# An account of VectorE's work paces the convolution's taps, pairs step first, and VectorE copies the histories

## The chip, the cores and the metric

The kernel runs on one core of a Trainium2 chip. The core's engines run side by side, each through its own queue in order: TensorE (PE, with its weight loads as PEld), VectorE (DVE), ScalarE (ACT), GpSimd (POOL) and SyncE (SP), which issues the DMAs. The metric is the device time of one execution in microseconds; the lower the better.

## The reference, cut to what matters

One layer of a streaming encoder is computed for 320 tokens: 256 of a prompt and 64 of a running stream, with model width 2048.

```python
h = rmsnorm(x, g_pre_mix)
p = h @ w_in                                   # 6160 columns
a_out, conv_buf = conformer_conv(p[..., :c0], p[..., c0:c1], conv_buf, w_dw, b_dw, gn_g, gn_b)
b_out, qkv_buf, s = gdn_mixer(p[..., c1:c2], p[..., c2:c3], ...)   # 8 heads of 128, gated delta rule
x = x + rmsnorm(jnp.concatenate([a_out, b_out], axis=-1) @ w_out, g_post_mix)
h = rmsnorm(x, g_pre_ffn)
gu, ffn_buf = causal_dwconv(h @ w_up, ffn_buf, w_ffn_dw, b_ffn_dw)
x = x + rmsnorm((jax.nn.silu(gate) * up) @ w_down, g_post_ffn)
```

The part that the change touches is the Conformer convolution: a gated input `u = h_val * sigmoid(h_gate)`, then a causal depthwise convolution over positions with 31 taps, each output needing the 30 positions before it (its history: zeros, or for the running stream a stored state), then a group norm over 128 channels and a swish. Eight groups of 128 channels are eight independent convolutions. The other half is the gated delta rule: per head a short convolution of q, k and v, and a blockwise recurrence in chunks of 64 or 128 tokens with the inverse of a triangular matrix.

## The kernel before, in words

All activations lie with channels on the 128 partitions and the 320 tokens along the free axis. Each weight matrix is cut into blocks of 128 output channels. A block's weights arrive by DMA in two half blocks of 1024 columns (three buffers). ScalarE rounds a half block to a high part (`whi`, line L214) and VectorE computes the rest (`wlo`, L215); TensorE then makes three products for each 128 rows (L230, L231, L234): high by high, high by low, low by high. `block_matmul` does this, and each matmul is counted by `tick`. A block of the input projection has 16 x 3 = 48 ticks.

**The dense plan.** After the first norm, the string PLAN orders the blocks: `h0` to `h7` are heads (q, k and v block each: `gdn_pre`, `qkv_block`), `c0` to `c7` convolutions (gate block and value block: `conv_block`), `z0` to `z7` output gates. Then come the blocks of the output projection (`w_out1`, 33 ticks each), a second part of it (`w_out2`, L1051 to L1053), and the feed-forward layer, which has no part in the change.

**The jobs.** The small work between the blocks is written as Python generators, the jobs. A job yields at each point where its next matmuls would wait for other engines, and names how many ticks later it wants to go on, and how many PSUM banks of two kinds it holds. After every 20 ticks (GAP), `tick` opens a slot: it takes the jobs that are due, in order of their due time, as far as the banks go, and lets each issue its next step right behind the dense matmul. A step that yields with the word "scale" is taken after the others. The jobs are

- `conv_tail` of each convolution: it looks once per slot whether its taps are issued, then transposes (L575), takes statistics (L577 to L584), scales (`un`, L588), transposes back (L592) and applies the swish (`af`, L594, `bh`, L238);
- `gdn_tail` of each head: transposes of q, k and v (L673 to L677), squares on ScalarE (L679, L681), norms on GpSimd (L686 to L692), scaled copies (L696 to L701), and the products `pk` and `pks` (L705, L709) with VectorE's `np` and `at` (L713, L717). Its last step marks the head as done;
- `pair` of each two heads: it looks once per slot whether both heads are marked; `base_inverse` then stores `np` by SP's queue (L729) and inverts small blocks on VectorE (L744 to L758); `levels` widens the inverse in steps of TensorE and ScalarE (`pz` L782, `zh` L783, `px` L788, again with `zq` L807 and `px` L812); `post` runs the recurrence (`pvn` L854, `po` L862, `rhs` L875, `pvns` L883) and ends in `pt_o` (L937) and `zo` (L939).

**The convolution's taps.** `conv_block` evaluates the gate (`sg`, L533) and value (`hv`, L540) and writes `ub` (L541), a tile of five segments of 94 columns: 30 of history and 64 new. ScalarE then copies the stored state and the other segments' histories (L543, L544). `ub` has three buffers, so convolution b takes that of b - 3. The convolution is 31 multiply-adds over 320 columns on VectorE (L557 to L560, in two sums `cvt` and `odd`) and one addition (L554): 32 instructions, which `conv_block` puts into the list `taps`. At the end of a slot `tick` issues the first few of the list, ordered behind the newest VectorE instruction of the slot's jobs. How many is `pace`: 1 while a head's blocks run, 3 in other steps of the plan, 4 after it. `finish_conv(b - 3)` issues what is left of an older convolution before its buffer is written again, and after the plan convolutions 0 to 4 are finished, since `w_out1` reads them.

The order on each engine is set when the program is built: instructions go by their place in the program, minus an offset for those inside `high_priority` (evacuations of PSUM 3000, jobs 1500, weight splits 600, taps none), as their buffers and inputs allow.

Of the kernel before, what the change touches and what calls it, by code (L numbers as in the profile page):

```python
# [22 lines left out]
T = TP + TS  # L23
# [5 lines left out]
HALF = 1024  # L29
NWARM = 8  # L30
GAP = 20
PRI_J = 1500
LAG_GATE = 60
LAG_CONV = 40
# [65 lines left out]
@with_exitstack  # L100
def trunk_kernel(ctx, tc, ins, outs):
    nc = tc.nc
    V, S, G, PE = nc.vector, nc.scalar, nc.gpsimd, nc.tensor
    PRI_W = 600
    boost = [0]
    PRI_E = 3000
# [3 lines left out]

    dense = [None, 0]
    held_t = [0]
    jobs = []


    taps, pace = [], [3]

    def next_tap(front=None):
        left, fn = taps.pop(0)
        with ExitStack() as e:  # L120
            if front is not None:
                e.enter_context(tc.issue_after(front))
            fn()
        left[0] -= 1

    def advance(job, behind=None):
        with tc.issue_after(behind or dense[0]), tc.high_priority(offset=PRI_J):
            try:
                wait, job[2], job[3], *kind = next(job[1])
                job[0] = dense[1] + wait  # L130
                job[4] = kind
            except StopIteration:
                jobs.remove(job)
        return next(i for i in reversed(nc.cur_bb.bb.instructions) if i.engine == dense[0].engine)

    def start(gen, wait, g=0, t=0):
        job = [dense[1] + wait, gen, g, t, []]
        jobs.append(job)
        return job
# [5 lines left out]
    def newest(engine, n0):  # L145
        return next((i for i in reversed(nc.cur_bb.bb.instructions[n0:]) if i.engine == engine), None)

    def tick(mm):
        dense[0] = mm.ins
        dense[1] += 1  # L150
        if dense[1] % GAP == 0:
            g, t0, behind, due = 0, held_t[0], dense[0], []
            t = t0
            n0 = len(nc.cur_bb.bb.instructions)
            for job in sorted(jobs, key=lambda j: j[0]):
                if job[0] <= dense[1] and g + job[2] <= 4 and t + job[3] <= 2:
                    g += job[2]
                    t += job[3]
                    due.append(job)
            for job in due:  # L160
                if not job[4]:
                    behind = advance(job, behind)
            scalar = newest(mybir.EngineType.Activation, n0)
            for job in due:
                if "scale" in job[4]:
                    with ExitStack() as e:
                        if scalar is not None:
                            e.enter_context(tc.issue_after(scalar))
                        advance(job)
            held_t[0] = t - t0  # L170
            front = newest(mybir.EngineType.DVE, n0)
            for _ in range(min(pace[0], len(taps))):
                next_tap(front)

    const = ctx.enter_context(tc.tile_pool(name="const", bufs=1))
# [13 lines left out]
    def pv(name, a=None, b=None):  # L189
        o, w = PAR[name]  # L190
        if a is None:
            return par[:, o:o + w]
        return par[:, o + a:o + (a + 1 if b is None else b)]
# [103 lines left out]
    def in_block(b, name):  # L297
        if b in ready:
            return ready.pop(b)
        ps = ps_p.tile([P, 512], F32, tag="p", name=name)  # L300
        block_matmul(ps[:, 0:T], ins["w_in"][b], hx, (8, 8))
        return ps
# [10 lines left out]
    with tc.tile_pool(name="xp", bufs=1) as xp:  # L313
# [85 lines left out]
        def first_norm():  # L399
            rr, _ = rstd([ssum[:, 0, :], ssum[:, 1, :]])  # L400
            yield 36, 1, 0
            S.copy(rb, rstd_rows(rr)[0])

        job = start(first_norm(), 24, 1)
# [116 lines left out]
    def finish_conv(b):  # L521
        while any(left is lefts[b] for left, _ in taps):
            next_tap()
        finish(convs[b])
# [3 lines left out]
    def conv_block(b):  # L528
        psg_ = in_block(8 + b, "psgate")
        ub = ubufs[b % 3]  # L530
        with tc.high_priority(offset=PRI_E):
            sg = cb.tile([P, T], F32, tag="sg", bufs=1, name="sg")
            V.tensor_tensor(sg, psg_[:, 0:T], rb, ALU.mult)  # L533
            S.activation(sg, sg, AF.Tanh, scale=0.5)
        psv = in_block(b, "psv")
        if b > 2:
            finish_conv(b - 3)
        with tc.high_priority(offset=PRI_E):
            hv = cb.tile([P, T], F32, tag="t320", bufs=2, name="hv")
            V.scalar_tensor_tensor(hv, psv[:, 0:T], 0.5, rb, ALU.mult, ALU.mult)  # L540
            V.scalar_tensor_tensor(ub[:, :, 30:94], sg.rearrange("p (s i) -> p s i", s=5), 1.0,  # L541
                                   hv.rearrange("p (s i) -> p s i", s=5), ALU.add, ALU.mult)
            S.copy(ub[:, 4, 0:30], pv("s_conv", b * 30, (b + 1) * 30))  # L543
            S.copy(ub[:, 1:4, 0:30], ub[:, 0:3, 64:94])  # L544
        for i in range(2):
            nc.sync.dma_start(outs["conv"][:, b, i, :], ub[:, 3 + i, 64:94])

        cvt = cb.tile([P, 5, 64], F32, tag="cvt", bufs=3, name="cvt")
        odd = cb.tile([P, 5, 64], F32, tag="odd", bufs=1, name="odd")
        left = [32]  # L550

        def tap(t):
            if t == 31:
                return lambda: V.tensor_tensor(cvt, cvt, odd, ALU.add)  # L554
            x, acc, w = ub[:, :, t:t + 64], (cvt, odd)[t % 2], pv("w_dw", b * 31 + t)
            if t == 0:
                return lambda: V.tensor_scalar(acc, x, w, pv("b_dw", b), ALU.mult, ALU.add)  # L557
            if t == 1:
                return lambda: V.tensor_scalar(acc, x, w, None, ALU.mult)
            return lambda: V.scalar_tensor_tensor(acc, x, w, acc, ALU.mult, ALU.add)  # L560

        lefts[b] = left
        taps.extend((left, tap(t)) for t in range(32))
        return cvt.rearrange("p s i -> p (s i)"), left

    def conv_tail(b, cvt, left):
        while left[0]:
            yield GAP, 0, 0
        yield LAG_CONV, 0, 1
# [79 lines left out]
    def gdn_tail(h, st, kq, vT):  # L649
        s = h % NS  # L650
        while not gate or (s and "kq" not in st) or (h // NS > 1 and "free" not in sts[h // NS - 2]):
            yield GAP, 1 + 2 * s, 1
        if s == 0:
# [72 lines left out]
    def base_inverse(bt, st):  # L726
# [9 lines left out]
        G.memset(wi_t[:, 0:256:17], 1.0)  # L736
        yield 2 * GAP, 0, 0

        d8, w8 = (t.rearrange("p (b x) -> p b x", b=2)[:, :, 0:128].rearrange("p b (r c) -> p b r c", c=16)[:, :, :, 0:8]
                  for t in (dn_t, wi_t))  # L740
        for r in range(6, -1, -1):
# [5 lines left out]
            if r in (3, 0):  # L747
                yield GAP, 0, 0
        tmp = tmp_t.rearrange("p (r c s) -> p r c s", r=8, c=8)
# [3 lines left out]
        V.tensor_reduce(x, tmp, AX.X, ALU.add)  # L753
        yield GAP, 0, 0
        V.tensor_tensor(tmp, wi[:, 0:8, 0:8].unsqueeze(2).to_broadcast((nb, 8, 8, 8)),
# [195 lines left out]
    def pair(i, st):  # L951
        while any(s not in st for s in range(NS)):
            yield GAP, 0, 0
        yield from base_inverse(i, st)
        yield LAG_BASE - 5 * GAP, 1, 0
        yield from levels(st)
        while i and any(j is pairs[i - 1] for j in jobs):
            yield GAP, 2, 0
        yield LAG_WAIT, 2, 0
        yield from post(i, st)  # L960

    plan = PLAN.split()
    tails, convs, pairs, sts = {}, {}, {}, []
    for step in plan:
        kind, i = step[0], int(step[1:] or 0)
        pace[0] = 1 if kind == "h" else 3
        if kind == "c":
            convs[i] = start(conv_tail(i, *conv_block(i)), GAP)
        elif kind == "g":
            gates_job = start(gates(), 0)  # L970
            advance(gates_job)
        elif kind == "h":
            if i % NS == 0:
                if i:
                    ready[24 + i] = in_block(24 + i, "psq")
                st = {}
                sts.append(st)
                pairs[i // NS] = start(pair(i // NS, st), 0)
            tails[i] = start(gdn_tail(i, st, *gdn_pre(i, st)), LAG_HEAD, 1 + 2 * (i % NS), 1)
        else:  # L980
            z_block(i)
    pace[0] = 4
    for i in range(5):
        finish_conv(i)
    for i in range(3):
# [8 lines left out]
    for n in range(KB - 1):  # L994
        psm = ps_p.tile([P, 512], F32, tag="p", name="psm")
        block_matmul(psm[:, 0:T], ins["w_out1"][n], bx, (6, 5))
        m.append(act.tile([P, T], F32, tag=f"hl{n}", name=f"m{n}"))
        with tc.high_priority(offset=PRI_E):
            S.copy(m[n], psm[:, 0:T])
    while jobs:  # L1000
        advance(jobs[0])
    pa.close()
# [107 lines left out]
    first = up_group()  # L1110
# [13 lines left out]
    job = start(second_norm(), 68, 1)  # L1124
# [29 lines left out]
    for q in range(NQ):  # L1154
# [5 lines left out]
        for j in range(QB):  # L1160
            b = q * QB + j
# [53 lines left out]
    for step in PLAN_Y.split():  # L1215
        how, ks = step[0], step[1:]
        n = 2 if len(ks) == 4 else 1
# [96 lines left out]
```

## Time and profile before

| | |
|---|---|
| median of 3 runs | 1500.84 us (1497.14 to 1501.93) |
| the profiled execution | 1498.26 us, of it the span 1496.5 us |
| TensorE busy | 1480.7 us (99%), 10609 matmuls |
| VectorE busy | 998.4 us (67%) |
| ScalarE busy | 723.7 us (48%) |
| GpSimd busy | 226.4 us (15%) |
| mean granted TensorE clock | 0.998 |

The span is the time from the first to the last instruction that the profiler recorded. A row of an engine's timeline gives its start from the span's beginning, its length, the source line, what it writes and reads, and in square brackets how long the engine stood idle before it and what it waited for. A row of waits gives the engine, what it was about to write, what it waited for, and then the total in us, the number of times and the longest. Lengths of neighbouring rows overlap, since an engine starts an instruction before the one ahead has wholly ended; the distance of two starts is what an instruction costs its queue. L215 and the like are lines of the kernel before.

### The profile page before, as it was taken

Reading aid. Unit: us, or ns where it says so; the run is one execution under the profiler, and the core shown is the slowest. Engines: PE = TensorE matmul, PEld = TensorE weight load, DVE = VectorE, ACT = ScalarE, POOL = GpSimd, SP = SyncE. Lnnn points to the kernel's source line nnn. Section 1 sums busy time; section 2 is a strip of 40 time slices with the busy share of each in tenths; the row PEclk is TensorE's granted clock in tenths of the full one; section 3 lists DMA queues with packets and bytes.
Section 4 is the critical chain, followed back from the end, with each engine's and each line's share of the span. In section 5 each row is a group of like instructions: output and inputs, shape, how many; then the busy total and the mean of one; then the engine's idle time right before and its main releaser. Section 6 shows DMA issues by size and latency. Waiting matters only on the chain.

```text
span 1496.5 us, 27233 instructions
## 1 busy us (share of the span) xinstructions
PE 1480.7 (99%) x10609; PEld 1459.7 (98%) x10610; DVE 998.4 (67%) x1840; ACT 723.7 (48%) x1305; POOL 226.4 (15%) x390
## 2 busy tenths in 40 slices
PE   9999999999999999999999999999999999999998
PEld 8999899989999999999999999999999999999997
DVE  6779886979989678766335666445666545656554
ACT  7664556554544656544434444334444333444453
POOL 0011001120010000332002222002223101223101
PEclk9999999999999999999999999999999999999999
DMA  8435453444434744444554444454444455444453
GB/s 297 134 128 160 137 157 120 131 143 144 130 106 142 226 146 141 154 143 130 154 166 154 149 151 137 138 159 162 152 155 138 136 149 171 154 147 150 131 151 118
DMA packets 98281, 224.22 MB, mean 150 GB/s; under 512 B 18792, under 2 KB 39528, under 8 KB 98152
## 3 DMA queue, kind: packets, MB, share of 16 engines
q1 hardware_dynamic: 98008, 222.45, 47.4%
q8 instruction: 83, 1.36, 0.4%
q14 instruction: 46, 0.38, 0.1%
q10 hardware_dynamic: 144, 0.03, 0.0%
HBM read 215.33 MB, written 7.12 MB: 149 GB/s over the span
## 4 chain that ended last, share of the span: by engine, by line
PE 82%; DVE 9%; ACT 3%; DMA 2%; issue 2%; POOL 1%; ACTq 0%; DVEq 0%; POOLq 0%
PE psu L234 13%; PE psu L231 13%; PE psu L230 13%; PE psdn L230 7%; PE psdn L231 6%; PE psdn L234 6%; DVE wlo L215 3%; PE psq L230 3%; PE psq L231 3%; PE psq L234 3%; PE psu L1107 1%; ACT whi L214 1%; DVE cvt L560 1%; PE ps_first L395 1%; DMA w<-in_w_out 1%
## 5 line engine op out<-in xcount | busy, mean ns | idle before, releaser
L214 ACT CAST whi<-w 128x1024 fp32r<-128x1024 f32 (+2 forms) x440 | 412.9, 940 | 488.4 <-PE psu L231 169.4
L215 DVE TENSOR_TENSOR wlo<-w,whi 128x1024 fp32r<-128x1024 f32 (+2 forms) x440 | 477.3, 1085 | 196.5 <-ACT whi L214 124.7
L231 PE MATMUL psu<-lo,whi 128*128 128x320 f32 x1344 | 397.0, 309 | 0.0
L230 PE MATMUL psu<-hi,whi 128*128 128x320 f32 x1344 | 397.0, 309 | 0.0
L231 PEld LDWEIGHTS psu<-lo,whi 128*128 128x128 f32 x1344 | 252.3, 188 | 0.0
L230 PEld LDWEIGHTS psu<-hi,whi 128*128 128x128 f32 x1344 | 252.3, 188 | 0.0
L234 PE MATMUL psu<-hi,wlo 128*128 128x320 f32 x1344 | 224.4, 309 | 0.0
L234 PEld LDWEIGHTS psu<-hi,wlo 128*128 128x128 f32 x1344 | 204.0, 188 | 0.0
L231 PE MATMUL psdn<-gl,whi 128*128 128x320 f32 x660 | 195.9, 310 | 0.0
L1140 POOL COPY nffn<-fbuf 128x2 f32<-128x2 f32 x88 | 101.5, 1153 | 586.9 <-DVE fbuf L1138 583.7
L1138 DVE TENSOR_TENSOR fbuf<-psu,rb 128x256 f32<-128x256 f32 x88 | 37.4, 425 | 168.9 <-PE psu L234 168.9
L230 PE MATMUL psdn<-gh,whi 128*128 128x320 f32 x480 | 142.8, 309 | 0.0
L231 PEld LDWEIGHTS psdn<-gl,whi 128*128 128x128 f32 x660 | 123.9, 188 | 0.3
L230 PE MATMUL psq<-hh,whi 128*128 128x320 f32 x352 | 106.2, 315 | 0.0
L231 PE MATMUL psq<-hl,whi 128*128 128x320 f32 x352 | 104.1, 309 | 0.0
L230 PEld LDWEIGHTS psdn<-gh,whi 128*128 128x128 f32 x480 | 90.1, 188 | 0.0
L234 PE MATMUL psdn<-gh,wlo 128*128 128x320 f32 x480 | 89.9, 309 | 0.0
L234 PEld LDWEIGHTS psdn<-gh,wlo 128*128 128x128 f32 x480 | 75.3, 188 | 0.0
L230 PEld LDWEIGHTS psq<-hh,whi 128*128 128x128 f32 x352 | 66.1, 188 | 0.3
L231 PEld LDWEIGHTS psq<-hl,whi 128*128 128x128 f32 x352 | 66.1, 188 | 0.2
L560 DVE SCALAR_TENSOR_TENSOR cvt<-ub,par,cvt 128x320 f32<-128x320 f32 x120 | 65.3, 545 | 0.2
L1183 DVE TENSOR_TENSOR y<-y,psdn 128x320 f32<-128x320 f32 x45 | 22.0, 488 | 58.9 <-PE psdn L234 58.9
(357 smaller groups left out, 2479.5 us busy)
## 6 DMA issues: line engine op xcount, KB each, us to landing
w<-in_w_up SPq DMA_DIRECT2D x176, 512.0 KB, 3.6
w<-in_w_in SPq DMA_DIRECT2D x88, 512.0 KB, 3.9
w<-in_w_down SPq DMA_DIRECT2D x64, 384.0 KB, 3.2
w<-in_w_down SPq DMA_DIRECT2D x64, 320.0 KB, 2.9
w<-in_w_out SPq DMA_DIRECT2D x32, 320.0 KB, 3.3
w<-in_w_out SPq DMA_DIRECT2D x16, 384.0 KB, 3.1
w<-in_w_first SPq DMA_DIRECT2D x6, 512.0 KB, 6.5
wtp<-wsp SPq DMA_DIRECT2D x4, 640.0 KB, 5.8
```

Source lines behind the costliest of these rows:

```text
L214: S.copy(hi[:, 0:width], w[:, 0:width])
L215: V.tensor_tensor(lo[:, 0:width], w[:, 0:width], hi[:, 0:width].bitcast(F32), ALU.subtract)
L230: tick(PE.matmul(ps, wh, xh, start=(first and k0 + j == 0), stop=False))
L231: tick(PE.matmul(ps, wh, xl, start=False, stop=False))
L234: tick(PE.matmul(ps, lo[:, j * P:(j + 1) * P], xh, start=False, stop=(final and k0 + j == nk - 1)))
L395: tick(PE.matmul(ps, w, xh, start=(k == 0 and wt is hi), stop=(k == KB - 1 and wt is lo)))
L560: return lambda: V.scalar_tensor_tensor(acc, x, w, acc, ALU.mult, ALU.add)
L1107: PE.matmul(pss[i][:, 0:T], wt[:, o:o + P], x, start=(k == 0 and n == 0), stop=(k == KB - 1 and n == 2))
L1138: V.tensor_tensor(buf[:, 2:258], psu[:, 0:TP], rb2[:, 0:TP], ALU.mult)
L1140: G.tensor_copy(nffn[:, b, 0, :], buf[:, 256:258])
L1183: V.tensor_tensor(y[:, n, :], y[:, n, :], psd[:, 0:T], ALU.add)
```

## The change

- **The account.** All VectorE instructions go through a wrapper, `Counted`, which adds 0.12 us plus 0.00094 us per column to `spent`. At the end of a slot the account's `ends` (when VectorE would be done) is raised to the slot's start if it lies behind it, and `spent` is added; `clock` moves on by V_SLOT = 3.1 us. Taps are then issued as long as the next one would still end by `clock`. The fixed `pace` is gone, in the plan and after it; before the last jobs are run out, all taps that are left are issued.
- **Pairs first.** Of the due jobs of a slot, the pairs' steps are issued first; the choice of the due jobs stays as it was.
- **The histories.** The two copies into `ub` (L543, L544) are VectorE's instead of ScalarE's.

```diff
+V_OP, V_COL = 0.12, 0.00094
+V_SLOT = 3.1
...
-    V, S, G, PE = nc.vector, nc.scalar, nc.gpsimd, nc.tensor
+    S, G, PE = nc.scalar, nc.gpsimd, nc.tensor
+    spent = [0.0]
+    class Counted:
+        def __getattr__(self, name):
+            fn = getattr(nc.vector, name)
+            def run(out, first, *args, **kw):
+                n = first.free_size() if name in ("tensor_reduce", "bn_stats") else out.free_size()
+                spent[0] += V_OP + n * V_COL
+                return fn(out, first, *args, **kw)
+            return run
+    V = Counted()
...
-    taps, pace = [], [3]
+    taps, clock, ends = [], [0.0], [0.0]
...
-            for job in due:
+            for job in sorted(due, key=lambda j: all(j is not p for p in pairs.values())):
                 if not job[4]:
                     behind = advance(job, behind)
...
-            for _ in range(min(pace[0], len(taps))):
+            ends[0] = max(ends[0], clock[0] - V_SLOT) + spent[0]
+            clock[0] += V_SLOT
+            spent[0] = 0.0
+            while taps and ends[0] + spent[0] + V_OP + T * V_COL <= clock[0]:
                 next_tap(front)
...
-            S.copy(ub[:, 4, 0:30], pv("s_conv", b * 30, (b + 1) * 30))
-            S.copy(ub[:, 1:4, 0:30], ub[:, 0:3, 64:94])
+            V.tensor_copy(ub[:, 4, 0:30], pv("s_conv", b * 30, (b + 1) * 30))
+            V.tensor_copy(ub[:, 1:4, 0:30], ub[:, 0:3, 64:94])
...
-        pace[0] = 1 if kind == "h" else 3
...
-    pace[0] = 4
...
+    while taps:
+        next_tap()
     while jobs:
         advance(jobs[0])
```

More of the change, by code (lines that the diff above doesn't have):

```diff
@@ L112, in trunk_kernel @@
     held_t = [0]
-    jobs = []
-    taps, pace = [], [3]
+    jobs, pairs = [], {}
+    taps, clock, ends = [], [0.0], [0.0]
     def next_tap(front=None):
@@ L962, in trunk_kernel @@
     plan = PLAN.split()
-    tails, convs, pairs, sts = {}, {}, {}, []
+    tails, convs, sts = {}, {}, []
     for step in plan:
         kind, i = step[0], int(step[1:] or 0)
-        pace[0] = 1 if kind == "h" else 3
         if kind == "c":
```

## The prediction

> **What bounds the kernel now.** I read the page first, then the busy time by stretch, then the waits of TensorE, and last the order of instructions around each of its waits.
>
> ```profile
> span 1496.5 us, 27233 instructions
> ...
> PE 1480.7 (99%) x10609; PEld 1459.7 (98%) x10610; DVE 998.4 (67%) x1840; ACT 723.7 (48%) x1305; POOL 226.4 (15%) x390
> ```
>
> TensorE is busy for 99% of the span, and the change removes no matmul. All that can be won is TensorE's idle time, and only where the scheduled jobs run, before about 500 us. The next rows are stretches there (us; busy time of PE, PEld, DVE, ACT, POOL; granted clock; DMA), then one plain stretch from the second half of the layer.
>
> ```profile
> core 0: us, PE busy (x) PEld busy (x) DVE busy (x) ACT busy (x) POOL busy (x), PEclk, DMA share, GB/s
> ...
> 151.91:186.53 34.62, 32.53 (x355) 30.84 (x354) 28.93 (x70) 18.40 (x51) 3.60 (x9) 0.95 0.42 136
> ...
> 263.18:308.73 45.55, 45.55 (x313) 45.14 (x312) 39.98 (x88) 24.84 (x68) 8.23 (x19) 1.00 0.50 144
> 308.73:325.37 16.64, 14.65 (x203) 14.14 (x201) 15.74 (x38) 8.32 (x28) 2.02 (x2) 1.00 0.48 164
> 325.37:420.95 95.58, 93.06 (x827) 89.42 (x826) 80.78 (x174) 48.49 (x116) 8.62 (x15) 1.00 0.42 125
> 420.95:500.00 79.05, 78.32 (x548) 78.03 (x547) 68.18 (x146) 36.82 (x77) 6.90 (x14) 1.00 0.46 133
> ```
>
> ```profile
> 840.00:880.00 40.00, 40.00 (x275) 40.00 (x274) 26.39 (x45) 18.02 (x23) 11.93 (x18) 1.00 0.45 148
> ```
>
> Undisturbed, a matmul takes 40/275 = 0.1455 us, so a slot of 20 lasts 2.91 us. TensorE stands still for 2.09, 1.99, 2.52 and 0.73 us in the four stretches with a gap, 7.3 us in all. Its waits (us in total, times, longest) name them:
>
> ```profile
> PE px L788 <- ACT zh L783: 4.5, 3, 2.1
> ...
> PE pvns L883 <- DVE rhs L875: 1.4, 1, 1.4
> PE pt_o L937 <- ACT un L588: 0.7, 1, 0.7
> PE px L812 <- ACT zq L807: 0.6, 1, 0.6
> ...
> PE psm L1051 <- ACT m L999: 0.3, 1, 0.3
> PE psm L1051 <- ACT bh L238: 0.3, 1, 0.3
> ```
>
> The largest is the level step of a pair: TensorE makes `pz`, ScalarE scales it to `zh`, TensorE multiplies `zh` into `px` one slot later. `zh` is short; it is late because of what stands before it in ScalarE's queue. The first such wait, ScalarE's order and then TensorE's:
>
> ```profile
> 155.51 0.22 ACT L543 COPY ub<-par 128x30 f32<-128x30 f32 x1 [1.12 <-DVE odd L560]
> 155.63 1.04 ACT L214 CAST whi<-w 128x1024 fp32r<-128x1024 f32 x1
> 156.58 0.27 ACT L679 ACTIVATE vh<-tkq 128x128 f32<-128x128 f32 x1
> ...
> 158.47 0.35 ACT L783 ACTIVATE zh<-pz,cst 128x80 f32<-128x80 f32 x1
> ```
>
> ```profile
> 158.87 0.30 PE L788 MATMUL px<-wtp,zh 32*16 32x16 f32 x19 [2.09 <-ACT zh L783]
> ...
> 160.36 0.47 PE L230 MATMUL psz<-hh,whi 128*128 128x320 f32 x1
> ...
> 163.29 0.46 PE L231 MATMUL psz<-hl,whi 128*128 128x320 f32 x1
> ```
>
> ScalarE stood 1.12 us at the history copy (it waits for the last tap that reads the buffer's earlier tenant), then did the tail's squares, 156.58 to 158.47 = 1.89 us, and only then `zh`. Behind the wait the clock fell: 12 matmuls start between 160.36 and 163.29, 0.266 us apart, which costs 12 x 0.12 = 1.5 us. That is the 0.95 in the first stretch; so this one event is worth 2.09 + 1.5 = 3.6 us. [...]
>
> The second wait has another cause:
>
> ```profile
> 316.71 0.42 ACT L630 ACTIVATE vT<-cq 128x256 f32<-128x256 f32 x1 [1.11 <-DVE cq L628]
> ...
> 317.18 0.31 ACT L783 ACTIVATE zh<-pz,cst 128x80 f32<-128x80 f32 x1
> ```
>
> Here `zh` stands behind a SiLU of the last q/k/v block, which waits for VectorE. The third, for `pvns`, waits for VectorE itself, whose order was
>
> ```profile
> 350.73 1.07 DVE L755 TENSOR_TENSOR tmp<-wi,dn 40x512 f32<-40x512 f32 x1
> 351.71 0.48 DVE L533 TENSOR_TENSOR sg<-psgate,rb 128x320 f32<-128x320 f32 x1
> 352.23 0.36 DVE L875 SCALAR_TENSOR_TENSOR rhs<-ks,neG,vh 64x128 f32<-64x128 f32 x1
> ```
>
> **Part 1, the account.** It prices a tap at 0.12 + 320 x 0.00094 = 0.42 us and a weight split at 1.08 us. VectorE's own starts, with no idle time between:
>
> ```profile
> 152.95 0.54 DVE L560 SCALAR_TENSOR_TENSOR cvt<-ub,par,cvt 128x320 f32<-128x320 f32 x1
> 153.41 0.47 DVE L533 TENSOR_TENSOR sg<-psgate,rb 128x320 f32<-128x320 f32 x1
> 153.81 1.21 DVE L215 TENSOR_TENSOR wlo<-w,whi 128x1024 fp32r<-128x1024 f32 x1
> 154.94 0.54 DVE L560 SCALAR_TENSOR_TENSOR odd<-ub,par,odd 128x320 f32<-128x320 f32 x1
> ```
>
> A tap costs 0.46 us and a split 1.13, so the account is 9% and 4% low, and its slot of 3.1 stands for about 3.3 us of VectorE in a real slot of 2.91 plus the jobs' matmuls. What that does in the stretch 263.18 to 308.73 (14 slots; heads 6 and 7, one tap per slot before), where the taps of L560 are these (DVE busy, count):
>
> ```profile
> 263.18:308.73 45.55, 8.04 (x16) 1.00 0.50 144
> ```
>
> VectorE's other work is 39.98 - 16 x 0.46 = 32.6 us, about 30.6 in the account's prices (x 0.94). The budget is 14 x 3.1 = 43.4; 12.8 are left, or 30 taps instead of 16. Really that is 32.6 + 30 x 0.46 = 46.4 us in 45.55: VectorE full. The same sum over the other stretches of heads gives 10 to 18 taps more in each, so convolutions end earlier, fewer taps stand in the convolutions' and pairs' late stretches, and I estimate 22 fewer left at the end of the plan: at 4 to 5 a slot, the last convolution's sum comes about 5 slots, 15 us, before this row:
>
> ```profile
> 487.10 0.48 DVE L554 TENSOR_TENSOR cvt<-cvt,odd 128x320 f32<-128x320 f32 x1
> ```
>
> The gains from it: the two 0.3 us waits of L1051 at 500 us (the last convolution's `bh`, and the copy beside it) go, -0.6. Around 312 us conv 2's taps are done, four or five fewer (2 us) stand before the SiLU's `cq`; around 350 us likewise two, which with the shift below takes 1.0 of the 1.4 us off `pvns` (bounds 0 to -1.4). The wait of `pt_o` for a statistic's PSUM bank moves with its convolution: -0.5 (0 to -0.7).
>
> Its cost is VectorE's backlog in the head stretches. What is late then is a split, and TensorE behind it; the shortest lead there is
>
> ```profile
> 289.24 1.24 DVE L215 TENSOR_TENSOR wlo<-w,whi 128x1024 fp32r<-128x1024 f32 x1
> ```
>
> ```profile
> 291.98 1.19 PE L234 MATMUL psq<-hh,wlo 128*128 128x320 f32 x7
> ```
>
> The split ends at 290.48, 1.5 us before its use. In six bare slots in a row the backlog grows 6 x (3.3 - 2.91) = 2.3 us, 0.8 more than the lead; two such places cost +1.6 at most by this, 0 if the jobs' matmuls stretch the slots; I take +1.2. Were the cover gone altogether, each further tap would cost its 0.46 us.
>
> **Part 2, pairs first.** On ScalarE it takes squares from before `zh`, 1.89 us in the first wait. But it also moves the chain. A pair that waits for its heads looks once per slot. A tail's last step (30 matmuls after the one before) falls due earlier than the pair's look, so before it ran first and the pair started in the same slot; now the pair looks first, finds nothing, and starts a slot later. All four chains move 2.9 us against the dense blocks, DMAs too. The first of them, the store of `np`, stands in SP's queue before weight loads and waits for VectorE:
>
> ```profile
> SPq L729 <- DVE np L717: 2.9, 4, 1.0
> ```
>
> A slot later those 2.9 us go from SP; TensorE did not feel them: 0. Nothing needs a chain's end that soon: the last `zo` is over by 450 us and used at 500.
>
> For the waits: at 156 the squares are done a slot before `pz`, so all 3.6 us go (bounds 0 and -3.6). At 315 `px` comes due near 318.2 while `zh` ended at 317.5; it can go wholly, or trip the clock as at 160 (+1.5); I take -1.5. The third `zh` wait (4.5 - 2.09 - 1.99 = 0.4) would then stand behind a gate's evacuation: -0.1, bounds -0.4 and +0.4. The `zq` wait loses squares ahead, but TensorE also reaches a pair's matmul sooner, without the tail's matmuls before it: -0.3, bounds -0.6 and +1.3; for the same loss of cover elsewhere +0.6.
>
> **Part 3, the copies.** ScalarE no longer waits here (us, times, longest):
>
> ```profile
> ACT ub L544 <- DVE ub L541: 7.6, 6, 2.2
> ...
> ACT ub L543 <- DVE odd L560: 3.3, 3, 2.0
> ```
>
> Those 10.9 us are head-of-line time of an engine that is 48% busy; they reach TensorE only at 156 us, counted above. On VectorE sixteen copies, each near this row (64 columns),
>
> ```profile
> L624 DVE TENSOR_TENSOR qb<-psq,rb 128x64 f32<-128x64 f32 x18 | 3.9, 217 | 0.0
> ```
>
> cost 16 x 0.2 = 3.2 us over 340 us. They need no wait of their own there: 0 on TensorE, bounds 0 and +0.4 (one conv's pair of copies).
>
> **The sum.** -3.6 - 1.5 - 0.1 - 0.3 - 1.0 - 0.5 - 0.6 = -7.6; +1.2 + 0.6 = +1.8; net -5.8. The profiled execution took 1498.26 us (its span and 1.8 around it): 1492.5. The runs shown go from 1497.14 to 1501.93, their median 2.6 above it; I add about half and forecast **1494 us**.
>
> **Rivals.**
> - *The waits move and stay.* Chains shifted by a slot meet other evacuations; three of four `zh` steps had no margin before, and each shifted one can meet a `cq` or `sg` in the same way. For it: ScalarE's order at 317. Against: the squares and the copy's wait are certain to leave. What goes at 156 (-3.6) comes back elsewhere (+1.99 and the costs of +1.8): 1498.5 against the same execution, 1499.5 by the median.
> - *VectorE is overbooked: slower.* In the three long head stretches (84 to 152, 187 to 238, 263 to 309) the backlog passes the splits' lead by 2 us, TensorE waits for `wlo` and the clock halves: 3 x (2.0 + 1.5) = +10.5, with -3.6 kept: 1505, 1506 by the median. It decides from a backlog of 1.5 + 2.0 = 3.5 us at a place like 292 us; my arithmetic gives 2.3. [...]
> - *The account does little.* A tap's place on VectorE also follows what else is ready, and conv blocks already ran at three a slot; if the order hardly moves and the shift cancels out, 1500.
>
> **Chances.** Forecast 0.60 (own range 1489 to 1497.5), waits that stay 0.22, overbooked 0.13, little 0.05. A measurement tells about 0.3%, 4.5 us, from no change: faster is below 1496.3, slower above 1505.3. Of the forecast 0.52 is faster and 0.08 same; of the second 0.04 and 0.18; the last is same; of the overbooked 0.12 slower. Faster 0.56, same 0.32, slower 0.12. The range goes from all waits gone (7.3 + 1.5 + 0.6 less a little, 1488) up to most of the second rival and not the third: 1488 to 1503.
>
> **What would show it.** Right: `px` no longer waits 2 us for `zh`; no stretch below clock 1.00 before the end; some 30 taps between heads 6 and 7 instead of 16; the last tap near 470; no ScalarE wait at a history copy; the store of `np` no longer waits for VectorE. Wrong: TensorE waits for `wlo` in the stretches of heads (account too generous), or for `zh` and `zq` at new places (shift), or the last tap stays near 487 (account idle).

## The result, and the profile after

The changed kernel takes **1502.65 us** (median of 20 runs, 1499.74 to 1506.29) where the kernel before took 1499.19 in the same comparison. The ratio is 1.0027, with a 95% interval of 1.0020 to 1.0034: some 4 us slower, where 1494 was forecast. Its profiled execution took 1502.01 us. Line numbers are some 20 higher than before, and all of VectorE's instructions now carry L116, the line of the wrapper.

The page of the changed kernel: span, and busy time by engine.

```profile
span 1500.2 us, 27229 instructions
...
PE 1483.0 (99%) x10609; PEld 1461.9 (97%) x10610; DVE 998.0 (67%) x1856; ACT 721.9 (48%) x1289; POOL 233.3 (16%) x390
```

VectorE has as much to do as before and ScalarE 1.8 us less. GpSimd, whose work the change does not touch, is busy 6.9 us longer. TensorE's waits up to 560 us (total, times, longest):

```profile
PE px L808 <- ACT zh L803: 4.4, 2, 3.1
PE pks L729 <- ACT vh L721: 4.0, 1, 4.0
...
PE pt_c L595 <- DVE cvt L116: 0.7, 1, 0.7
...
PE tkq L693 <- DVE zo L116: 0.3, 1, 0.3
PE px L832 <- ACT zq L827: 0.2, 1, 0.2
PE pt_o L957 <- ACT un L608: 0.2, 1, 0.2
```

And two stretches behind the two largest (us, length, busy time and instructions of PE, PEld, DVE, ACT and POOL, granted clock, DMA):

```profile
112.10:119.00 6.90, 5.52 (x20) 5.34 (x21) 3.00 (x8) 4.37 (x11) 1.03 (x5) 0.51 0.12 24
330.50:334.00 3.50, 3.50 (x15) 3.50 (x14) 2.82 (x7) 2.27 (x6) 0.00 (x0) 0.51 0.45 123
```

The waits for `pvns`, for `bh` and `m` at 500 us and the 2.09 us at 156 us are gone. In their place stand 4.0 us for `pks`, a product of a head's tail that did not wait before, and 3.1 us for `zh`; the clock is halved behind both. In sum TensorE's waits before come to 8.3 us (7.8 in the rows shown ahead, and 0.5 for `wlo` at L1053) and those here to 9.8, each without the two at the start and at the second norm, which stand in both. The halved clock cost 1.5 us before and costs about half of 5.52 + 3.50 here, 4.4. That is +4.4 us, against +3.7 between the spans; the other 0.7 I can't assign.

**The 4.0 us at 109 us.** VectorE's taps in 92 to 104 us, first in the sum `odd`, then in `cvt`, in the changed kernel:

```profile
92.00:104.00 12.00, 4.37 (x8) 1.00 0.41 133
...
92.00:104.00 12.00, 3.83 (x7) 1.00 0.41 133
```

and the same two in the kernel before:

```profile
92.00:104.00 12.00, 0.00 (x0) 1.00 0.39 132
...
92.00:104.00 12.00, 1.10 (x2) 1.00 0.39 132
```

The account issues 15 taps there instead of 2. Short work of the first heads runs in that stretch. GpSimd's norm of the first head, then that of the second and one of its following steps, after the change:

```profile
101.64 3.11 POOL L706 TENSOR_TENSOR sc<-tq,nhalf 128x4 f32<-128x4 f32 x1 [30.09 <-ACT tq L704]
...
109.37 1.38 POOL L706 TENSOR_TENSOR sc<-tq,nhalf 128x6 f32<-128x6 f32 x1 [3.26 <-ACT tq L704]
...
110.99 1.52 POOL L709 TENSOR_TENSOR sc<-sc,kdec 128x3 f32<-128x3 f32 x1
```

before, where VectorE was idle:

```profile
101.38 1.04 POOL L686 TENSOR_TENSOR sc<-tq,nhalf 128x4 f32<-128x4 f32 x1 [30.09 <-ACT tq L684]
```

and ScalarE, then TensorE, after the change:

```profile
105.68 0.37 ACT L716 ACTIVATE kd<-tkq,sc 128x128 f32<-128x128 f32 x1 [3.19 <-POOL sc L709]
...
113.06 0.37 ACT L721 ACTIVATE vh<-tv,sc 128x128 f32<-128x128 f32 x1
```

```profile
113.48 1.22 PE L729 MATMUL pks<-kqs 128*128 128x256 f32 x2 [4.02 <-ACT vh L721]
```

The norm takes 3.11 us instead of 1.04. ScalarE stands 3.19 us for it with the second head's squares queued behind, so the second norm is late too, then `vh`, then TensorE.

**The 3.1 us at 325 us.** VectorE, then ScalarE, then TensorE:

```profile
320.72 0.55 DVE L116 SCALAR_TENSOR_TENSOR cvt<-ub,par,cvt 128x320 f32<-128x320 f32 x1
...
323.03 0.55 DVE L116 TENSOR_TENSOR qb<-psq,rb 128x256 f32<-128x256 f32 x2
...
324.63 0.55 DVE L116 SCALAR_TENSOR_TENSOR cq<-qb,par,cq 128x323 f32<-128x323 f32 x1
325.10 0.54 DVE L116 SCALAR_TENSOR_TENSOR odd<-ub,par,odd 128x320 f32<-128x320 f32 x1
325.56 0.55 DVE L116 SCALAR_TENSOR_TENSOR cq<-qb,par,cq 128x323 f32<-128x323 f32 x1
```

```profile
327.07 0.42 ACT L650 ACTIVATE vT<-cq 128x256 f32<-128x256 f32 x1 [1.78 <-DVE cq L116]
...
328.47 0.32 ACT L803 ACTIVATE zh<-pz,cst 128x80 f32<-128x80 f32 x1
```

```profile
328.84 0.46 PE L808 MATMUL px<-wtp,zh 32*16 32x16 f32 x38 [3.11 <-ACT zh L803]
```

Five taps (320.72 to 323.03, 2.31 us) stand before the evacuation `qb`, and one more between each two of the three steps of `cq` (0.46 us each). ScalarE's SiLU `vT` waits for `cq`, and `zh` stands behind it. The seven taps together take 3.2 us, as long as the wait.

### The profile page after: what moved, and what is told of

It reads as the page before. It is cut to its first block, busy times and chain, and to the rows that moved or that the text cites. A ratio compares the mean times of both kernels' runs of the same rounds, so it can differ in the third digit from the quotient of the medians.

```text
span 1500.2 us, 27229 instructions
## 1 busy us (share of the span) xinstructions
PE 1483.0 (99%) x10609; PEld 1461.9 (97%) x10610; DVE 998.0 (67%) x1856; ACT 721.9 (48%) x1289; POOL 233.3 (16%) x390
## 4 chain that ended last, share of the span: by engine, by line
PE 90%; DVE 3%; ACT 3%; POOL 2%; issue 1%; DMA 0%; SPq 0%; ACTq 0%; DVEq 0%
PE psu L254 13%; PE psu L251 13%; PE psu L250 13%; PE psdn L250 7%; PE psdn L251 6%; PE psdn L254 6%; PE psq L250 2%; PE psq L251 2%; PE psq L254 2%; PE psm L251 2%; PE psm L250 2%; PE psm L254 2%; PE psu L1127 1%; PE ps_first L415 1%; PE psv L250 1%; PE psv L254 1%
## 5 line engine op out<-in xcount | busy, mean ns | idle before, releaser
L116 DVE TENSOR_TENSOR wlo<-w,whi 128x1024 fp32r<-128x1024 f32 (+3 forms) x450 | 487.4, 1083 | 203.8 <-ACT whi L234 127.3
L1160 POOL COPY nffn<-fbuf 128x2 f32<-128x2 f32 x88 | 98.3, 1117 | 586.7 <-DVE fbuf L116 585.9
L116 DVE TENSOR_TENSOR fbuf<-psu,rb 128x256 f32<-128x256 f32 (+1 forms) x176 | 48.5, 319 | 170.1 <-PE psu L254 170.1
L116 DVE SCALAR_TENSOR_TENSOR cvt<-ub,par,cvt 128x320 f32<-128x320 f32 x120 | 65.2, 543 | 0.3
L116 DVE SCALAR_TENSOR_TENSOR odd<-ub,par,odd 128x320 f32<-128x320 f32 x112 | 60.9, 544 | 0.4
```

What stands on the lines that cost most here:

```text
L116: return fn(out, first, *args, **kw)
L1160: G.tensor_copy(nffn[:, b, 0, :], buf[:, 256:258])
```

## The experiments

Ratios are to the kernel before, with 95% intervals. The theory at first: the account puts taps where short work of VectorE and GpSimd is awaited. Rivals: the new order costs, or the copies do. In the quoted expectations, theory G says that a run of taps holds GpSimd's norm and so costs, B that VectorE is simply booked too full, S that the shifted chains of the pairs cost.

**Which part?** One part undone each time, then parts alone.

```diff
 # e1_no_pairs_first
-            for job in sorted(due, key=lambda j: all(j is not p for p in pairs.values())):
+            for job in due:
 # e2_no_account
-            while taps and ends[0] + spent[0] + V_OP + T * V_COL <= clock[0]:
+            for _ in range(min(pace[0], len(taps))):     # 1, 3 and 4, as before
 # e3_scalar_copies
-            V.tensor_copy(ub[:, 1:4, 0:30], ub[:, 0:3, 64:94])     # and the other
+            S.copy(ub[:, 1:4, 0:30], ub[:, 0:3, 64:94])
 # g1_pairs_first_alone, j1_copies_alone: that part alone put into the kernel before
```

> The changed kernel with the jobs again in order of their due time alone; account and copies stay. Theory G (the account's unbroken run of taps after the first convolution stretches GpSimd's norm from 1.04 to 3.11 us, ScalarE waits for it, and TensorE waits 4.0 us for a PSUM bank at pks, with a halved clock behind): nothing of that depends on the order of pairs, so the 4.0 us wait near 109 us and two halved windows stay; 1500 to 1504 us. Theory S (the one-slot shift of the pairs' chains is what costs, by the two waits of px for zh at 226 and 325 us, 1.5 and 3.1 us plus a halved window): these two go and the time falls to about 1497, below the kernel before.

> The changed kernel with the fixed numbers of taps per slot (1, 3, 4) again; pairs first and the copies on VectorE stay. Theory G: GpSimd's first norm takes about 1.0 us again, no wait at pks, no halved clock at 112 us; the wait before px at 156 us stays away; 1493 to 1496 us, faster than both kernels. Theory S: the waits of px near 226 and 325 us stay, so 1498 to 1501.

> The changed kernel with the two history copies on ScalarE again; account and pairs first stay. Both theories: the 4.0 us wait at pks stays, ScalarE waits at the copies up to 10 us again as before but TensorE hardly feels it; 1500 to 1505 us, within 2 us of the changed kernel. If the copies on VectorE were what costs, it would fall to 1499 or below.

> The kernel before with the pairs' steps first in a slot and nothing else: fixed pace of the taps, histories copied by ScalarE. Theory 'the order is the gain' (the wait at 156 us goes because the squares no longer stand before zh): 1491, within 2 us of the kernel with order and copies (1489.9), and px's two waits of 2 us are gone. Rival 'the copies are needed too' (ScalarE's stand of 1.1 us at a history copy stays ahead of zh and of other work): 1495, with px <- zh still at 1 us or more at some place. Rival 'they only move' : 1498 to 1500.

> The kernel before with the histories copied by VectorE and nothing else. Theory 'the stand at the copy is only a part of the wait at 156 us' (the squares stay ahead of zh): 1497 to 1499, px <- zh near 156 us 1 us shorter, with or without the halved clock behind it. Rival 'the copies alone undo it' (ScalarE's 1.1 us suffice for zh to come within the clock's patience): 1494 to 1496, no halved clock near 160 us.

| account | pairs first | copies | us | ratio, interval |
|---|---|---|---|---|
| no | yes | no (g1) | 1492.44 | 0.9958, 0.9945 to 0.9972 |
| no | no | yes (j1) | 1497.10 | 0.9983, 0.9974 to 0.9991 |
| no | yes | yes (e2) | **1489.89** | 0.9941, 0.9926 to 0.9955 |
| yes | no | yes (e1) | 1498.41 | 0.9997, 0.9988 to 1.0006 |
| yes | yes | no (e3) | 1506.08 | 1.0048, 1.0032 to 1.0063 |
| yes | yes | yes | 1502.65 | 1.0027, 1.0020 to 1.0034 |

The account costs 12.8 us beside the other two parts, which without it make the kernel 8.8 us faster (0.0059 of 1498.6). That version beats both kernels. Without pairs first the account costs 1.3 us by the medians (2.1 by the ratios): the parts do not add up. The traces say where they meet. The wait for `pks` stands in e1 (3.29 us) and e3 (4.02) as in the changed kernel, and in none of the three without the account, so it comes of the account in any order of the jobs. The wait of 3.11 us for `zh` needs the new order too: in e1 the longest for `zh` is 1.05 us. In e3 2.81 us for `cvt` stand at that place, with the clock halved as well (its mean over the span is 0.996, as in the changed kernel).

The numbers expected were met only in part: e2 came out below both theories, e1 between them, and g1 between its theory and its rival. e3 lies 1 us above its range: beside the account the copies are worth some 3 us, not nothing, though the two intervals just overlap. TensorE's waits in e2, but for the two of the start and the second norm that stand in every kernel, and with no halved clock there (its mean over the span is 1.000):

```profile
PE px L846 <- ACT zq L842: 0.8, 1, 0.8
...
PE px L832 <- ACT zq L827: 0.5, 1, 0.5
PE psm L1075 <- DVE wlo L116: 0.5, 1, 0.5
PE psm L1073 <- ACT m L1019: 0.4, 1, 0.4
PE psm L1073 <- ACT bh L258: 0.3, 1, 0.3
```

They come to 2.5 us against 9.8, and the clock's 4.4 us is gone: 11.7 of the 12.2 us between the spans (1488.0 and 1500.2). Set side by side at the same dense matmul, the changed kernel falls 6.8 us behind e2 at the wait for `pks` and some 4 more at that for `zh`, is 14 to 15 us behind from 340 to 430 us and 12.4 at 560. The first norm and the first `kd` in e2:

```profile
101.29 1.04 POOL L706 TENSOR_TENSOR sc<-tq,nhalf 128x4 f32<-128x4 f32 x1 [30.09 <-ACT tq L704]
```

```profile
102.79 0.37 ACT L716 ACTIVATE kd<-tkq,sc 128x128 f32<-128x128 f32 x1 [0.65 <-POOL sc L709]
```

The copies alone take the wait at 156 us from 2.09 us to 0.15, with no halved clock behind it (the plain matmuls from 158.67 us on start 0.15 us apart):

```profile
157.24 0.46 PE L788 MATMUL px<-wtp,zh 32*16 32x16 f32 x38 [0.15 <-ACT zh L783]
```

So the mechanism that their rival named holds, yet the time moved by 2.5 us by the ratio (2.9 by the medians) and not by 3.6, and 1497.10 lies in the range of the theory, not of the rival.

**Is it GpSimd, held by the taps?** Four edits of the changed kernel: no tap before a given matmul, which clears the first norm; no tap in a slot with a norm pending; the taps of one sum put into the list after those of the other, so that each would wait for the one before; and prices and a bare slot as the trace shows them.

```diff
 # e4_late_taps
+            while taps and dense[1] >= 640 and ends[0] + ...
 # e5_no_tap_at_norm
+            while taps and not any("scale" in j[4] for j in jobs) and ends[0] + ...
 # f2_chained_taps
-        taps.extend((left, tap(t)) for t in range(32))
+        taps.extend((left, tap(t)) for t in (*range(0, 31, 2), *range(1, 31, 2), 31))
 # f1_true_prices
+V_OP, V_COL = 0.155, 0.00095
+V_SLOT = 2.91
```

> The changed kernel, in which no tap is issued before tick 640 (about 108 us), so the first convolution's taps do not run while the first two heads' norms are on GpSimd. Theory G: GpSimd's norm of the first head takes about 1.0 us, the 4.0 us wait at pks and the halved clock at 112 us go; 6 us less, about 1496. If instead VectorE is simply overbooked, the same taps come later, between 108 and 150 us, and make a wait of 2 us or more there; 1500 or above.

> The changed kernel, in which no tap is issued in a slot at whose end a job waits for GpSimd's norm (a step marked scale). Theory G: GpSimd's norms of the heads take 1.0 to 1.5 us, the wait at pks goes, 1494 to 1498 us. Theory B: the same work is only moved by a slot; the waits for cvt and zh stay, 1500 to 1504.

> The changed kernel with the taps in another order: all even ones first, then all odd ones, so that each waits for the one before it on VectorE and 35 ns stay free between them; as many taps at the same places. Theory G: GpSimd's first norm falls from 3.1 us to 1.6 or less, the 4.0 us wait at pks goes, 5 to 7 us less: 1496 to 1498. Theory B: VectorE has 8 us more to do and is later everywhere: 1503 to 1510.

> The changed kernel with the account's prices taken from the starts in the trace (0.155 us and 0.00095 per column: a tap 0.46, a split 1.13) and a slot of 2.91 us. Theory B: TensorE's waits for cvt at pt_c and for zh behind cq go, since no more is issued than VectorE can do: 1490 to 1495 us. Theory G: the run of taps right after the first convolution is still eight long or so, GpSimd's first norm still takes about 3 us and the wait at pks stays with its halved clock: 1496 to 1501.

Late taps gave 1500.95 (1.0014, 1.0005 to 1.0022): the first norm is back at 1.04 us and the wait for `pks` gone, but 3.0 us of `pt_c <- cvt` near 158 us and 3.1 of `px <- zh` near 324 came, and another norm took 4.91 us:

```profile
125.64 4.91 POOL L706 TENSOR_TENSOR sc<-tq,nhalf 128x4 f32<-128x4 f32 x1 [16.27 <-ACT tq L704]
```

Slots without taps at a norm gave 1502.34 (1.0020, 1.0009 to 1.0030) and no less waiting; the taps beside the first norm had been issued in slots before it. Chained taps gave 1508.59 (1.0055, 1.0042 to 1.0068): the first norm fell to 1.15 us and `pks`'s wait from 4.0 to 2.2, but two waits for `zh` came to 6.2. The edit did not do there what it was meant to: beside the first norm the taps of the two sums still follow each other in turn, as in the changed kernel.

```profile
101.59 1.15 POOL L706 TENSOR_TENSOR sc<-tq,nhalf 128x4 f32<-128x4 f32 x1 [30.09 <-ACT tq L704]
```

```profile
101.77 0.54 DVE L116 SCALAR_TENSOR_TENSOR odd<-ub,par,odd 128x320 f32<-128x320 f32 x1
102.23 0.54 DVE L116 SCALAR_TENSOR_TENSOR cvt<-ub,par,cvt 128x320 f32<-128x320 f32 x1
```

So this run does not show what chaining does for the norm; it shows a norm of 1.15 us beside the same kind of run that went with 3.11. With a norm 2.0 us shorter, `pks` waits 1.8 us less and still 2.2: the held norm is a part of the loss at 109 us, and not the whole of the loss.

The new prices gave 1531.17 (1.0206, 1.0192 to 1.0221), where both theories had 1501 or less: too few taps are issued, the last at 529 us, and TensorE waits for the convolutions' results:

```profile
PE pt_c L612 <- ACT un L608: 16.5, 4, 5.4
PE pt_c L595 <- DVE cvt L116: 4.0, 2, 2.5
```

This account is worse than the one whose prices are a little low. The edit changes two things, though: prices up, and the slot from 3.1 down to 2.91 us, while the 14 slots of the stretch from 263 to 309 us lasted 45.55/14 = 3.25 us each with the jobs' matmuls. Which of the two starves the convolutions was not tried apart.

**Where in the plan, and too many or too few?** The account capped at one tap per slot among heads' blocks (h1), or at work only there (h2); the account as a brake alone (i1) or as an addition alone (i2). All have pairs first and VectorE's copies.

```diff
 # h1_one_tap_in_heads
+            while taps and <account> and (pace[0] != 1 or n < 1):
 # h2_account_in_heads
+            while taps and (<account> if pace[0] == 1 else n < pace[0]):
 # i1_account_holds_back
+            while taps and n < pace[0] and <account>:
 # i2_account_adds
+            while taps and (n < pace[0] or <account>):
 # i3_holds_back_in_plan: i1, but after the plan four a slot in any case
 # k1_five_after_plan: e2 with pace[0] = 5 after the plan
```

> The changed kernel with the account, but at most one tap per slot while a head's blocks run, as before. Theory 'taps among the heads' blocks' (what the account costs is the work that it puts before q/k/v's convolutions and the norms): 1490 to 1492, pks no longer waits 4 us near 109 us and px no longer 3 us near 325 us. Rival 'the account's other slots' (uneven numbers of taps in the steps of convolutions and gates, and after the plan): 1500 to 1503.

> The reverse: the account gives out taps only while a head's blocks run; three taps a slot in the other steps and four after the plan, as before. Theory 'taps among the heads' blocks': 1501 to 1503, with pks waiting 3 us or more near 109 us. Rival 'the account's other slots': 1490 to 1492.

> The changed kernel, but a slot gets at most the taps of the fixed pace (1, 3, 4); the account can only hold taps back. Theory 'bursts' (the account costs where it gives out more taps than the fixed pace, right behind a convolution's blocks, and short work that other engines wait for stands in the burst): 1490 to 1493, like the changed kernel with the fixed pace (1489.9), and no wait of pks at 109 us. Rival 'held back' (the account costs where it gives out fewer, and taps pile up before a later slot): 1497 to 1503.

> The reverse: a slot gets at least the taps of the fixed pace, and more where the account has room. Theory 'bursts': 1500 to 1510, with pks waiting 3 us or more near 109 us. Rival 'held back': 1490 to 1493.

> As the kernel whose account can only hold taps back, but after the plan four taps a slot are issued whatever the account says. Theory 'its loss is the late end' (the taps held back in the plan are few; those held back after it came as late as 493 us and TensorE waited for the last convolutions' un and bh): 1490 to 1492, last tap near 480, pt_c <- un below 1 us. Rival 'the taps held back in the plan are themselves too late': 1496 to 1499.

> Fixed pace with pairs first and VectorE's copies (1489.9), with five taps a slot after the plan instead of four. Theory 'bursts cost only where heads' short work stands in them' (none is left after the plan): the last tap is some 8 us earlier and TensorE's two waits of 0.3 to 0.6 us near 492 us go, 1489 to 1490. Rival 'five a slot is a burst too': pt_o or pt_c waits 1 us or more between 410 and 480 us, 1491 to 1495.

| | us | ratio, interval |
|---|---|---|
| h1, one tap among heads | 1497.47 | 0.9989, 0.9980 to 0.9999 |
| h2, account among heads only | 1508.19 | 1.0067, 1.0053 to 1.0080 |
| i1, brake only | 1498.17 | 0.9987, 0.9978 to 0.9996 |
| i2, addition only | 1508.74 | 1.0057, 1.0043 to 1.0070 |
| i3, brake in the plan only | 1497.87 | 0.9981, 0.9971 to 0.9991 |
| k1, five after the plan | 1495.57 | 0.9975, 0.9963 to 0.9987 |

h1 came out between its theory and its rival, and h2 above both, with a wait for `pks` of 1.3 us where 3 or more was expected, and 3.1 us for `zq` and 4.4 for `cvt` instead. Against e2 the addition alone costs 18.9 us, the brake alone 8.3, and the account, which does both, 12.8. Where the account only adds, the waits of the changed kernel stand again, and more:

```profile
PE px L810 <- ACT zh L805: 4.4, 2, 3.1
PE pt_o L959 <- ACT un L610: 3.7, 2, 2.3
PE pks L731 <- ACT vh L723: 3.4, 1, 3.4
PE px L834 <- ACT zq L829: 3.1, 1, 3.1
```

Where it only brakes, all of these but 0.2 us for `zq` are gone, and others stand at the late end of the taps (the last at 493 us):

```profile
PE pt_c L614 <- ACT un L610: 4.3, 2, 2.5
...
PE psm L1075 <- ACT bh L260: 1.1, 1, 1.1
```

So the bursts make the waits for `pks` and `zh`, as the theory of bursts says; but 1490 to 1493 was expected of the brake and 1498 came. Set side by side with e2 at the same dense matmul, the brake's kernel is up to 1 us ahead until 409 us, and loses all of it behind that. i3 asked whether that loss comes only of the taps held back after the plan: TensorE's waits near 500 us shrank from 3.6 us (2.51 and 1.13) to 1.1 (0.95 and 0.18), the wait of 1.8 us for `un` at 412 us stayed, and the median moved by 0.3 us, so its rival held. In k1 two waits for the taps' sum came (`pt_c <- cvt`, 3.5 us), near 452 and 477 us: a burst costs after the plan too, where no head's work stands in it. One tap among heads leaves waits for `zq` (5.0 us), among others near 400 us, where `zq` stands in ScalarE behind three `un` that waited 4.88 us for a convolution's norm. The cost of the account is thus a matter of both signs: more taps in a slot than 1, 3 and 4 make short work late, fewer make the convolutions late. Both single directions, brake and addition, were run; which slots cost how much was not tried one by one.

**The held norm by itself.** The whole layer is left out; GpSimd's power operation beside stretches of VectorE work of one kind.

```diff
+G.tensor_tensor(sq[i][:, 0:4], prev[:, 0:4], nhalf[:, 0:4], ALU.pow)     # six times, beside
+V.scalar_tensor_tensor(acc[k], ub[:, :, i:i + 64], par[:, i:i + 1], acc[k], ALU.mult, ALU.add)
```

> Leaves the whole layer out (the outputs are zeros). Eight stretches one after the other; in each GpSimd does seven of its power operations (128x6) while VectorE does nothing (first and last), taps on two sums in turn, taps on one sum (each waits for the one before), splits of 1024 columns, products out of PSUM, copies, or products with a scalar. Theory G (an unbroken run of taps holds GpSimd off): about 1.0 us each beside nothing, 3 us or more beside taps in turn, under 1.6 beside taps on one sum, whose 35 ns gaps let GpSimd in. Theory B (VectorE is only booked too full, and GpSimd's long spans come of something else): about the same in all stretches.

> The whole layer is left out. Stretch by stretch GpSimd raises 4 columns to the power -0.5 six times, each from the one before, while VectorE runs alone nothing, then 24 taps of 320 columns as the convolution has them (in two sums, five segments), the same on plain columns, in one sum (each waits for the one before), in two sums with a read of PSUM at every sixth place, 10 weight splits, and 24 copies. Theory 'an unbroken run holds GpSimd': beside the taps in two sums the first power lasts until the run ends, 8 us or more; beside the run with PSUM reads 2 to 3 us; beside one sum and beside nothing 1.0 to 1.4 us. Rival 'only operations with one source hold it': beside all kinds of taps 1.0 to 1.5 us and beside the copies 6 us or more.

GpSimd ran ahead of the stretches in both, so the rows are matched by time; and the taps on one sum ran in turn with other stretches' work, so that no row stands beside them alone. In m2, beside the convolution's taps, then beside the same taps on plain columns, and the one after the run's end:

```profile
14.62 1.31 POOL L139 TENSOR_TENSOR sqstrided<-sqstrided,nhalf 128x4 f32<-128x4 f32 x1
...
24.57 11.85 POOL L139 TENSOR_TENSOR sqflat<-sqflat,nhalf 128x4 f32<-128x4 f32 x1
...
36.49 1.01 POOL L139 TENSOR_TENSOR sqflat<-sqflat,nhalf 128x4 f32<-128x4 f32 x1
```

```profile
24.37 11.18 DVE L151 SCALAR_TENSOR_TENSOR flat<-x,par,flat 128x320 f32<-128x320 f32 x24
```

Alone it takes 1.01 us, beside most runs 1.31, but one that started in the run of 24 plain taps lasted until 0.9 us after it. In m1, whose powers of 6 columns take 1.32 us alone, those beside plain taps took 1.42, and four beside copies and scalings 6.5 to 7.0. Neither theory holds: the kind of operation does not decide. What does is open.

## Why the prediction was wrong, and where it was right

- **The step that failed is the account's, in Part 1:** the cost of the backlog that it makes on VectorE, put at +1.2 us for late splits. The number of taps was a smaller fault. "30 taps instead of 16" was forecast for 263 to 309 us; the same dense matmuls ran from 267.12 to 316.03 us in the changed kernel, and these rows, `odd` and then `cvt`, show 20 there where both sums gave 17 before.

```profile
267.12:316.03 48.91, 5.36 (x10) 1.00 0.47 140
...
267.12:316.03 48.91, 5.42 (x10) 1.00 0.47 140
```

  For a part of it the list was empty: convolution 2's last tap ran at 261.85 us instead of 311.77, and convolution 3's first at 269.75. Why no more than 20 came is open beyond that. I had reckoned with a rate over whole stretches, and it is bursts: 15 taps in 92 to 104 us, five in a row from 320.72.
- **"What is late then is a split"** was wrong. TensorE waits nowhere for `wlo` in the changed kernel. Late is what has less lead and more hands: evacuations, convolution steps and norms that go from VectorE or GpSimd through ScalarE's queue to TensorE. The +1.2 us put there, with gains of 1.0, 0.5 and 0.6, made the account's part -0.9 us; it measures +12.8, of it 6.8 at the wait for `pks` and some 4 at that for `zh` (changed kernel against e2).
- **No account was taken of GpSimd.** Its norm took 3.11 us beside the taps against 1.04 with VectorE idle, which agrees with one engine holding up the other; the many powers of 1.31 us beside the same taps (m2) show no blocking for a whole run. What holds the norm is not shown.
- **The order and the copies** were right in sign and too small: -3.6 - 1.5 - 0.1 - 0.3 + 0.6 = -4.9 us against 8.8 measured. The wait at 156 us went as forecast, but each of the two parts undoes it alone, and the term for `pvns`, which I had shared with the account, belongs to the order: g1 does not have that wait.
- **The smaller gains of the account** came: the two waits at 500 us are gone, which stand in e2, and the last sum comes at 474.8 us instead of 487.1 (some 470 was forecast). `pt_o` fell from 0.7 to 0.2 us, but that is the order's: g1 and e2 do not have this wait.

```profile
474.78 0.49 DVE L116 TENSOR_TENSOR cvt<-cvt,odd 128x320 f32<-128x320 f32 x1
```

- **The pairs' chains** moved by one slot as forecast: counted in dense matmuls, the first `pz` of the four is 20, 20, 20 and 40 later. The store of `np` was to wait no longer for VectorE; it waits 4.5 us in four times instead of 2.9, without a wait of TensorE that I can trace to it.
- **The rivals.** "VectorE is overbooked" (1506) has the sign, is 3 us too high, and has not the mechanism: it decided from a split's lead at three places. "The waits move and stay" (1499.5) named the mechanism at 325 and 226 us, a shifted `zh` behind a `cq`; it lacked the bursts, which make `cq` late. Neither saw the two together, and without pairs first the account costs 1.3 to 2.1 us. "The account does little" is out: 15 taps ran for 2 in 92 to 104 us.
- **The clock.** To "trip the clock as at 160 (+1.5)" stood in the prediction as the other end of the second wait; that is what happened at 325 us, and for longer (2.7 us) at 109.

## What to carry to other kernels

An account of an engine's time says whether work fits, not who waits behind it: filling an engine as soon as there is room puts long work ahead of short work that three other engines wait for. Spread filler work, and look for the short steps that pass through the filled engine before raising its rate. Measure the parts of a change apart; here one part hid a gain of 8.8 us in the other two, and with prices nearer to the trace's and a shorter slot the account did worse (1531 us).

## What the hardware showed that was not expected

- GpSimd's power of 4 columns took 1.04 us with VectorE idle (before) and was seen at 3.11 (changed kernel) and 11.85 us (m2) beside unbroken runs of VectorE and at 4.91 in e4, but at 1.15 (f2) and 1.31 (m2) beside such runs too; the start alone doesn't tell which it will be.
- The wait that halved TensorE's clock had no fixed length. Single waits of 1.99 and 1.39 us (before), 1.98 (k1) and 1.31 (after) left it whole; 3.02 (e4), 3.11 and 4.02 us (after) halved it; between these both came about: 2.09 us (before) halved it, 2.26 (i2) did not. Two waits of the kernel with chained taps, and the clock behind each:

```profile
111.58 0.48 PE L729 MATMUL pks<-kqs 128*128 128x256 f32 x1 [2.17 <-ACT vh L721]
```

```profile
141.49 0.33 PE L595 MATMUL pt_c<-cst,cvt 128*128 128x128 f32 x1 [2.26 <-DVE cvt L116]
```

```profile
112.00:116.00 4.00, 4.00 (x20) 3.97 (x19) 1.97 (x5) 2.92 (x7) 0.00 (x0) 0.62 0.01 4
142.00:146.00 4.00, 4.00 (x30) 4.00 (x29) 3.96 (x10) 2.19 (x6) 0.00 (x0) 1.00 1.02 307
```

The shorter wait halved the clock (0.62) and the longer didn't (1.00). In i1 a wait of 1.83 us with one of 0.61 behind it halved it too (0.50 from 416.5 to 418.5 us).

  Where a wait lies seems to matter beside its length. The halved stretches of the two kernels last 3.41 us (before, 160.20 to 163.61; after, 330.52 to 333.93) or twice that (after, 112.07 to 118.89), and the two starts after lie 218.45 us apart, 64 times 3.413. In the 3.41 us ahead of each, TensorE stood still for 2.08 us (before), 2.61 (after, the wait for `pks`) and 1.73 (after, the wait for `zh`). This last wait had begun at 325.74 us: 1.37 of its 3.11 us lie ahead of 327.11, one step of 3.41 us before 330.52, and from 327.11 to 330.52 the clock was still whole (1.00). Of the 1.99 us before, 1.66 lie in one such step (313.80 to 317.21), and the clock behind it stayed at 1.00. So a halving agrees in these two traces with the time that TensorE stands still in a step of 3.41 us; these few steps give no limit.

  An estimate for the two waits with chained taps, from the rows above: a clock of 0.62 from 112 to 116 us stands for 3.04 us at half. If that is the front of a stretch, it begins at 112.96 us, some 2.0 of the 2.17 us lie in the step ahead of it, and the 2.26 us are split by the end of another step, 8 x 3.413 = 27.3 us later, into some 1.0 and 1.2.
